# S5 outputs with the inputs and carried states as stationary operands and the tables streaming 128 columns

## The chip, the cores and the metric

The kernel runs on one core of a Trainium2 chip. The metric is device microseconds of one execution, the median over several runs. TensorE is called PE in the profile (its weight loads PEld), VectorE DVE, ScalarE ACT, GpSimd POOL and SyncE SP.

## What is computed

A trunk of four layers over 256 tokens of 1024 channels; layers 0 and 3 mix tokens with a diagonal state-space model (S5), layer 1 with differential attention, layer 2 with causal pooling, and each is followed by a squared-ReLU MLP. The change touches the S5 mixer alone:

```
u = h @ w_in                                  # 256 tokens, 64 groups of 16 channels
x_t = abar * x_(t-1) + bbar @ u_t             # 64 complex states per group, abar and bbar from the parameters
y_t = Re(c @ x_t) + d_skip * u_t
z = gelu(y)
out = (z * sigmoid(z @ w_gate)) @ w_out
```

## The kernel before, in words

Everything is float32. The S5 layer is cut into four quarters of the channels, each of 16 groups, taken as eight pairs of groups, and the 256 tokens into 64 chunks of four tokens. A pair of groups (2 x 16 channels) times four tokens makes 128 rows, so that a chunk's inputs are one column `V[:, :, j]` of a [128, 64] operand. For each quarter the kernel makes tables from the parameters: S takes a chunk's inputs to the state that they reach, T a chunk's inputs to its own outputs, and O the state before a chunk to its outputs.

`SEQ` is the order of emission, written out by hand, and the matmuls of the layer are pinned to it. Its letters, each with a quarter: `g` the product with w_in, `V` its result in rows of channels, `i`, `o`, `s` the tables on the vector and scalar engines, `S` and `T` what TensorE makes of the tables (S by transposes, T by 16 small products with a 32-column stationary operand, here called the T fill, evicted at L623 and copied into place at L626), `m` the states (`s5_state`, 16 matmuls of 64 columns), `c` the states carried over the chunks (`s5_chain`, on the vector engine, ending in `h`), `y` the outputs (`s5_out`), `z` transposes of the GELU's result, `e` the gate product, `w` the product with w_out. In layer 3 the tables come from memory, where `s5_put` kept them (K, H, L bring them back).

The stage `y` stands at L708 to L731. For each of the eight pairs j it issues one matmul with T as the stationary operand (128 columns) and V streaming 64 columns, then two with the halves of O as stationary operand (64 columns each) and the carried state `h` streaming 64 columns; the two O products write the lower and the upper 64 rows of the same result. A float32 matmul is two instructions on the engine, so a stage is 48 instructions. The GELU (L725) then writes Z, which the vector engine turns in blocks of 32 (L729) so that `s5_z` (L734) can transpose it on TensorE. `s5_chain` (L683) makes the phase table with three rows (minus sine, cosine, sine) so that one add makes both parts, and its last four adds write `h` with the two groups of a pair side by side, 64 partitions at a time; `s5_out_table` (L632) copies O into place in four pieces of 64 partitions.

Two pools matter: `m2` (11 buffers) and `m4` (12 buffers); results of TensorE rotate through eight banks.

Of the kernel before, what the change touches and what calls it, by code (L numbers as in the profile page):

```python
# [39 lines left out]
def plan():  # L40
    """Half blocks of 256 rows x 512 columns (array, index, row, column) in the order in which they are used."""
# [50 lines left out]
class Net:  # L92
# [69 lines left out]
    def exp(self, out, x, shape, tag):  # L162
        """exp on the vector engine: 2^n times a polynomial of the rest, its even and its odd terms apart."""
# [26 lines left out]
    def fetch(self):  # L190
        """Loads and splits the half blocks [128, 2, 512] that come next."""
# [23 lines left out]
    def mm3(self, out, sh, sl, mh, ml, start, stop):  # L215
        """out += (sh + sl)^T (mh + ml), of which sl^T ml is below float32's rounding."""
# [6 lines left out]
    def gemm_unit(self, xT, u, banks, first, last):  # L223
        """Both token tiles times a half block of 256 x 512."""
# [14 lines left out]
    def gemm_quarter(self, xT, bank, first, last):  # L239
        """Both token tiles times 512 x 256, side by side in one bank."""  # L240
# [14 lines left out]
    def gemm_T_unit(self, xT, u, banks, first, last):  # L255
        """banks[f // 2][:, f % 2] += (half block of 256 x 512)^T xT for its four column tiles f."""
# [18 lines left out]
    def operand(self):  # L275
        """Half of an operand [512 channels, 256 tokens]: rounded part and the rest."""
        return tuple(self.m4([128, 4, NT, 128], F32R) for _ in range(2))

    def split_T(self, xT, src, t, scale=None):
        """xT[:, q, t] = src[:, 128 q:]^T (times scale[:, q]) for four q, split."""  # L280
# [11 lines left out]
    def stat(self, t, n):  # L292
        """The squares of x[t][:, n half] towards the mean square; after both, 1 / rms."""
# [15 lines left out]
    def normed(self, n, t, sub, delay=1.5):  # L309
        """x[t][:, n half] is final for sublayer sub: its operands and statistics."""  # L310
# [11 lines left out]
    def first(self, n):  # L322
        """The same for a half of the input, in whole operands."""
# [80 lines left out]
    def rounded(self, out, a, s):  # L404
        """The integer nearest to a * s."""
# [7 lines left out]
    def s5_parts(self, l, P, q):  # L413
        tb = P[q]
        return [tb["O"], tb["T"], tb["ph"][:, 1:3], tb["rho"]]

    def s5_put(self, l, q):
        """Keeps the tables in memory until their layer."""
# [8 lines left out]
    def s5_get(self, l, q, part):  # L427
        """Brings back the tables of one stage: states and inputs (0), carries (1), outputs (2)."""
# [4 lines left out]
        elif part == 1:  # L433
            ph = self.t([128, 3, 8, 64], "ph", 2)
            P[q].update(ph=ph, rho=self.t([128, 8, 64], "rho", 2))
            a = [ph[:, 1:3], P[q]["rho"]]
        else:
            a = [self.O[q % 2], self.T[q % 2]]
        d = P["kept", q]
        for a, d in zip(a, d[2:4] if part == 1 else d[0:2]):  # L440
            self.nc.sync.dma_start(out=a, in_=d)
        if part == 1:
            self.nc.scalar.mul(ph[:, 0], ph[:, 2], -1.0)

    def s5_params(self, l, P):
        """The discretised parameters, [128 = two groups x 64 states, 32 pairs of groups]."""
# [46 lines left out]
        # powers 4 .. 0 of the discretised eigenvalues, and the factor of the inputs  # L493
# [11 lines left out]
        self.cmul(pr[:, 1], pi[:, 1], pr[:, 2], pi[:, 2], pr[:, 3], pi[:, 3], [sm(f"v{q}") for q in range(4)])  # L505
# [39 lines left out]
    def products(self, b, wa, wb):  # L545
        """b[0] times wa and b[1] times wb: b [128, 8, 16] over columns and powers, wa and wb [128, 8, 2, 4] over channels."""
# [8 lines left out]
    def s5_in_table(self, l, P, q):  # L555
        """From the inputs of a chunk to its state, for the eight pairs of groups 8 q .. (S)."""
# [21 lines left out]
    def swapped(self, l, q):  # L578
        """Whether the table of the states goes through memory to be turned."""
        return l == 1  # L580

    def s5_late(self, l, q, d=None):
        """The parts of the tables that the tensor engine makes: S from the inputs to the state, T to the outputs."""
# [47 lines left out]
    def s5_out_table(self, l, P, q):  # L631
        """From the state before a chunk to its outputs."""  # L632
# [10 lines left out]
        for x in range(2):  # L643
            yield
            self.halves(lambda g, p: nc.scalar.copy(O[64 * x:64 * x + 64, :, g],
                                                    d[p, :, x, 1:5].rearrange("p j k h -> p j (k h)")))
        P[q]["d"] = d

    def s5_small_tables(self, l, P, q):
        """Phases of the chunks, e^{4 i theta (c - 32)}, and the decay over a chunk, zero where a pair begins."""  # L650
# [11 lines left out]
        ph = self.t([128, 3, 8, 64], "ph", 2)  # L662
        nc.scalar.activation(out=ph[:, 0], in_=f, func=AF.Sin, scale=-turn)
        nc.scalar.activation(out=ph[:, 1], in_=a, func=AF.Sin, scale=-turn, bias=self.hpi[:, 0:1])
        nc.scalar.activation(out=ph[:, 2], in_=f, func=AF.Sin, scale=turn)
# [6 lines left out]
    def s5_state(self, l, P, q, V):  # L672
        """Eight pairs: the states that the chunks reach, from zero."""
        tb = P[q]
        tb["sb"] = []
        for ri in range(2):
            ps = self.bank()
            for j in range(8):
                self.mm(ps[:, 64 * j:64 * j + 64], self.st[q % 2][:, :, 2 * j + ri], V[:, :, j], start=True, stop=True)
# [3 lines left out]
    def s5_chain(self, l, P, q):  # L683
        """Eight pairs: the states carried over the chunks, before each chunk."""
# [6 lines left out]
        for a in range(2):  # L691
            self.tt(m[a], sb[a].unsqueeze(1).broadcast_to(S), turn[:, a:a + 2], ALU.mult)
        self.tt(m[0], m[0], m[1], ALU.add)
        G = self.m4(S)
        fl = lambda a: a.rearrange("p j c -> p (j c)")
        for a in range(2):
            nc.vector.tensor_tensor_scan(out=fl(G[:, a]), data0=fl(tb["rho"]), data1=fl(m[0][:, a]), initial=0.0,
# [3 lines left out]
        for a in range(2):  # L701
            self.tt(m[a][:, :, :, w], G[:, a, :, w].unsqueeze(1).broadcast_to([128, 2, 8, 63]),
                    turn[:, a:a + 2, :, w], ALU.mult)
        tb["h"] = h = self.m4(S)
        nc.gpsimd.memset(h[:, :, :, 0:1], 0.0)
        for g in range(2):
            for x in range(2):
                p = slice(64 * g, 64 * g + 64)  # L708
# [548 lines left out]
```

## Time and profile before

| | |
|---|---|
| median of three runs | 1205.5 us (1204.42 to 1205.73) |
| span of the profiled execution, first to last instruction | 1204.5 us |
| PE busy in it | 1171.1 us (97%) |
| DVE, ACT, POOL busy | 809.9, 663.4, 52.3 us |
| mean granted clock of TensorE | 0.953 of full |

The page prints the span of the profiled execution; its own time is not among the answers of the trace, and the three runs lie between 0.1 us below and 1.2 us above the span. Busy time of PE overlaps itself (the ends of matmuls are modelled), so a stage is measured here from its first start to the first start of the next stage.

### The profile page before, as it was taken

To read this page: it belongs to the slowest core of one execution; us is meant where nothing else is said; L and a number is where in the kernel's file an instruction comes from. 1 tells how busy PE (TensorE), PEld (TensorE's weight loads), DVE (VectorE), ACT (ScalarE), POOL (GpSimd) and SP (SyncE) were. 2 spreads that over 40 slices of the span, in tenths; PEclk is the share of its full clock that TensorE was granted. 3 is DMA by queue.
4 is the path that set the end of the run, shared out by engine and by line. 5 is a ranking of instruction groups with operands and counts; after the bars stand their busy time and mean duration, and the time that the engine had idled before them with its cause. 6 is when DMAs were issued, how large, how long until landed. Compare 5 with 4: busy or idle time off the path is not lost.

```text
span 1204.5 us, 18922 instructions
## 1 busy us (share of the span) xinstructions
PE 1171.1 (97%) x7192; PEld 1042.7 (87%) x7192; DVE 809.9 (67%) x1488; ACT 663.4 (55%) x1322; POOL 52.3 (4%) x111
## 2 busy tenths in 40 slices
PE   5999999999999999999999999999999999999994
PEld 4989889899888788989888899899898889989983
DVE  7766579857658997986655765655764766655563
ACT  4846367656656676775644754544630156554452
POOL 4002000000000001000000100000100001000000
PEclk9877799999999999999999999999985799999998
DMA  5211256766665444667667365665542256556651
GB/s 150 88 35 36 84 179 188 228 219 208 207 208 168 140 143 154 198 207 217 192 189 232 98 201 180 186 185 185 174 132 79 89 172 195 183 182 189 183 185 58
DMA packets 56635, 196.51 MB, mean 163 GB/s; under 512 B 7136, under 2 KB 7648, under 8 KB 56544
## 3 DMA queue, kind: packets, MB, share of 16 engines
q1 hardware_dynamic: 54528, 189.69, 50.5%
q10 hardware_dynamic: 2016, 5.61, 1.4%
q8 instruction: 56, 0.92, 0.3%
q14 instruction: 35, 0.29, 0.1%
HBM read 188.46 MB, written 6.82 MB: 162 GB/s over the span
## 4 chain that ended last, share of the span: by engine, by line
PE 94%; ACT 2%; DMA 1%; DVE 1%; issue 0%; SPq 0%; POOL 0%; ACTq 0%; POOLq 0%
PE mlp_ps L142 60%; PE mix_ps L142 31%; PE mix_ps L146 2%; DMA start_raw<-in_wts 1%; ACT start_st L598 0%; PE mlp_ps L146 0%; ACT mix_m L885 0%; ACT start_T L626 0%; ACT start_T L623 0%; DVE mix_m L151 0%; SPq L1071 0%; ACT mlp_m L1170 0%; DVE start_x L151 0%; ACT start_ba L575 0%; ACT mix_m L794 0%
## 5 line engine op out<-in xcount | busy, mean ns | idle before, releaser
L151 DVE TENSOR_TENSOR mlp_wlo<-mlp_raw,mlp_whi 128x512 fp32r<-128x512 f32 x492 | 318.5, 686 | 215.9 <-ACT mlp_whi L204 215.7
L204 ACT CAST mlp_whi<-mlp_raw 128x512 fp32r<-128x512 f32 x492 | 281.5, 618 | 255.3 <-PE mlp_ps L142 190.9
L142 PE MATMUL mlp_ps<-mlp_whi,mlp_m 128*128 128x512 f32 x1024 | 327.8, 396 | 0.0
L142 PEld LDWEIGHTS mlp_ps<-mlp_whi,mlp_m 128*128 128x128 f32 x1024 | 192.8, 188 | 45.5
L142 PE MATMUL mlp_ps<-mlp_m,mlp_whi 128*128 128x256 f32 x1248 | 226.2, 283 | 0.0
L142 PE MATMUL mlp_ps<-mlp_wlo,mlp_m 128*128 128x512 f32 x512 | 202.9, 396 | 0.0
L142 PEld LDWEIGHTS mlp_ps<-mlp_m,mlp_whi 128*128 128x128 f32 x1248 | 192.1, 188 | 0.6
L142 PE MATMUL mlp_ps<-mlp_m,mlp_wlo 128*128 128x256 f32 x624 | 175.2, 281 | 0.0
L142 PE MATMUL mlp_ps<-mix_m,mlp_whi 128*128 128x256 f32 x672 | 122.1, 283 | 0.0
L142 PEld LDWEIGHTS mlp_ps<-mlp_m,mlp_wlo 128*128 128x128 f32 x624 | 118.3, 190 | 0.0
L142 PEld LDWEIGHTS mlp_ps<-mlp_wlo,mlp_m 128*128 128x128 f32 x512 | 96.5, 188 | 22.0
L142 PE MATMUL mix_ps<-mix_whi,mix_m 128*128 128x512 f32 (+1 forms) x352 | 108.7, 385 | 0.0
L151 DVE TENSOR_TENSOR mix_wlo<-mix_raw,mix_whi 128x512 fp32r<-128x512 f32 x124 | 81.5, 685 | 38.4 <-ACT mix_whi L204 38.3
L204 ACT CAST mix_whi<-mix_raw 128x512 fp32r<-128x512 f32 x124 | 72.6, 621 | 62.0 <-PE mix_ps L142 35.0
L142 PEld LDWEIGHTS mlp_ps<-mix_m,mlp_whi 128*128 128x128 f32 x672 | 104.5, 188 | 1.8
L142 PE MATMUL mlp_ps<-mix_m,mlp_wlo 128*128 128x256 f32 x336 | 94.5, 281 | 0.0
L142 PEld LDWEIGHTS mix_ps<-mix_whi,mix_m 128*128 128x128 f32 x352 | 66.3, 195 | 13.3 <-issue 0.5
L142 PE MATMUL mix_ps<-mix_wlo,mix_m 128*128 128x512 f32 (+1 forms) x176 | 67.1, 381 | 0.0
L151 DVE TENSOR_TENSOR mlp_m<-mlp_m,mlp_m 128x512 fp32r<-128x512 f32 (+1 forms) x72 | 51.5, 716 | 19.4 <-ACT mlp_m L360 18.6
L142 PEld LDWEIGHTS mlp_ps<-mix_m,mlp_wlo 128*128 128x128 f32 x336 | 63.8, 190 | 0.0
L142 PE MATMUL mix_ps<-mix_m,start_st 128*128 128x64 f32 x256 | 56.9, 398 | 0.4 <-ACT start_st L598 0.3
L142 PEld LDWEIGHTS mix_ps<-mix_m,start_st 128*128 128x128 f32 x256 | 56.4, 311 | 0.9 <-ACT start_st L598 0.9
(324 smaller groups left out, 1523.5 us busy)
## 6 DMA issues: line engine op xcount, KB each, us to landing
mlp_raw<-in_wts SPq DMA_DIRECT2D x252, 512.0 KB, 4.1
mix_raw<-in_wts SPq DMA_DIRECT2D x84, 512.0 KB, 3.6
kept<-mlp_m SPq DMA_DIRECT2D x4, 512.0 KB
start_st<-kept SPq DMA_DIRECT2D x32, 64.0 KB, 3.3
start_x<-in_x SPq DMA_DIRECT2D x4, 256.0 KB
start_raw<-in_wts SPq DMA_DIRECT2D x2, 512.0 KB, 16.8
mlp_m<-in_s5bc SPq DMA_DIRECT2D x2, 512.0 KB, 4.6
kept<-start_O ACTq DMA_DIRECT2D x2, 512.0 KB
```

The lines of the kernel that those rows point to most:

```text
L142: i = self.nc.tensor.matmul(*a, **k)
L146: i = self.nc.tensor.transpose(*a)
L151: (eng or self.nc.vector).tensor_tensor(out=out, in0=a, in1=b, op=op)
L204: nc.scalar.copy(hi[:, s], raw[:, s])
```

## The change

In `s5_out` the roles are exchanged: for two pairs at a time (r = 0, 1) the inputs V of a pair and the two parts of its carried state `h` (64 columns each) are stationary, and T and O stream 128 columns. Pair r = 0 writes the lower 64 rows of the result, pair r = 1 the upper 64; the matmuls alternate between them. The number of matmuls stays 24 a quarter. The result now has chunks in rows, so the GELU writes in the order that the transposes of `s5_z` read, and the two DVE turns are gone. `V` and `h` get a layout in which a pair's 64 columns lie side by side; `h` is written by two adds over 128 partitions, the phase table loses its row of minus sines, and `s5_chain`'s one add of 1024 columns becomes two of 512. O is block-diagonal over the two groups, twice as large and zeroed once at the start by POOL; it is filled by two copies a quarter of twice the size, and kept in memory as two halves. The rows of w_gate and w_out are permuted on the host to match. `pe(...)`, which counts TensorE time for deferred work, gets 0.65 for a group of six matmuls in place of 0.43 for three.

```diff
@@ s5_parts
-        return [tb["O"], tb["T"], tb["ph"][:, 1:3], tb["rho"]]
+        return [tb["O"][0:64, 0], tb["O"][64:128, 1], tb["T"], tb["ph"], tb["rho"]]
@@ s5_get
-            ph = self.t([128, 3, 8, 64], "ph", 2)
...
-        if part == 1:
-            self.nc.scalar.mul(ph[:, 0], ph[:, 2], -1.0)
@@ s5_out_table
-        for x in range(2):
-            yield
-            self.halves(lambda g, p: nc.scalar.copy(O[64 * x:64 * x + 64, :, g],
-                                                    d[p, :, x, 1:5].rearrange("p j k h -> p j (k h)")))
+        yield
+        self.halves(lambda g, p: nc.scalar.copy(O[p, g].rearrange("p j x k -> p (j x) k"),
+                                                d[p].rearrange("p j x k h -> p (j x) (k h)")[:, :, 16:80]))
@@ s5_small_tables
-        ph = self.t([128, 3, 8, 64], "ph", 2)
-        nc.scalar.activation(out=ph[:, 0], in_=f, func=AF.Sin, scale=-turn)
...
@@ s5_state
-                self.mm(ps[:, 64 * j:64 * j + 64], self.st[q % 2][:, :, 2 * j + ri], V[:, :, j], start=True, stop=True)
+                self.mm(ps[:, 64 * j:64 * j + 64], self.st[q % 2][:, :, 2 * j + ri], V[:, j], start=True, stop=True)
@@ s5_chain
-        self.tt(m[0], m[0], m[1], ALU.add)
+        self.tt(m[0][:, 0], m[0][:, 0], m[1][:, 1], ALU.add)
+        self.tt(m[1][:, 0], m[1][:, 0], m[0][:, 1], ALU.subtract)
...
-        for g in range(2):
-            for x in range(2):
-                p = slice(64 * g, 64 * g + 64)
-                self.tt(h[64 * x:64 * x + 64, g, :, 1:64], m[0][p, x, :, w], m[1][p, x, :, w], ALU.add)
+        self.tt(h[:, 0, :, 1:64], m[0][:, 0, :, w], m[1][:, 1, :, w], ALU.subtract)
+        self.tt(h[:, 1, :, 1:64], m[1][:, 0, :, w], m[0][:, 1, :, w], ALU.add)
@@ s5_out
-        for j in range(8):
-            o = ps[:, 64 * j:64 * j + 64]
-            self.mm(o, tb["T"][:, j].rearrange("p g x -> p (g x)"), V[:, :, j], start=True, stop=False,
-                    skip_group_check=True)
-            for g in range(2):
-                self.mm(o[64 * g:64 * g + 64], tb["O"][:, j, g], tb["h"][:, g, j], start=False, stop=g == 1,
+        for i in range(4):
+            o = [ps[64 * r:64 * r + 64, 128 * i:128 * i + 128] for r in range(2)]
+            for r in range(2):
+                j = 2 * i + r
+                self.mm(o[r], V[:, j], tb["T"][:, j].rearrange("p g x -> p (g x)"), start=True, stop=False,
                         skip_group_check=True)
-            self.pe(0.43)
-        Z = self.m2([128, NT, 8, 32])
-        nc.scalar.activation(out=Z.rearrange("p t j c -> p j t c"),
-                             in_=ps.rearrange("p (j t c) -> p j t c", j=8, t=NT), func=AF.Gelu_apprx_tanh)
-        z = self.m2([128, NT, 2, 128])
-        for t in range(NT):
-            nc.vector.transpose(out=z[:, t].rearrange("p k (j h) -> p j k h", j=8),
-                                in_=Z[:, t].rearrange("p j c -> p (j c)"))
-        tb["z"] = z
+            for x in range(2):
+                for r in range(2):
+                    j = 2 * i + r
+                    self.mm(o[r], tb["h"][:, x, j], tb["O"][:, :, j, x], start=False, stop=x == 1,
+                            skip_group_check=True)
+            self.pe(0.65)
+        tb["z"] = z = self.m2([128, 4, 8, 16])
+        nc.scalar.activation(out=z.rearrange("p s j h -> p j s h"), in_=ps.rearrange("p (j s h) -> p j s h", j=8, s=4),
+                             func=AF.Gelu_apprx_tanh)
@@ build
-        self.O = [self.t([128, 8, 2, 64], f"O{b}") for b in range(2)]
+        self.O = [self.t([128, 2, 8, 2, 64], f"O{b}") for b in range(2)]
...
-        for a in (self.ba[0], self.T[0], self.ba[1], self.T[1]):
+        for a in (self.ba[0], self.T[0], self.O[0], self.ba[1], self.T[1], self.O[1]):
             nc.gpsimd.memset(a, 0.0)
```

How the instructions move. First PE at the first output stage of layer 0 (`m1`, `y0`, then the T fill of quarter 1). A row names the result, the streaming operand and the stationary one, and the shape of the result; `st` are the tables S, `m_125` is V and `m_154` the carried state. Before:

```order
L142 MATMUL mix_ps_585<-mix_m_127_437,start_st_18_96 128x64 x8
L142 MATMUL mix_ps_621<-mix_m_125_431,start_T_21_99 128x64
L142 MATMUL mix_ps_621<-mix_m_154_570,start_O_19_97 64x64 x2
L142 MATMUL mix_ps_653<-mix_cad_475,start_ba_16_94 32x64 x16
L142 MATMUL mix_ps_676<-mix_raw_356,mix_m_24_107 128x256 x8
```

and now:

```order
L142 MATMUL mix_ps_580<-mix_m_127_438,start_st_18_96 128x64 x8
L142 MATMUL mix_ps_615<-start_T_21_99,mix_m_125_432 64x128 x2
L142 MATMUL mix_ps_615<-start_O_19_97,mix_m_154_567 64x128 x4
L142 MATMUL mix_ps_644<-mix_cad_475,start_ba_16_94 32x64 x16
L142 MATMUL mix_ps_667<-mix_raw_358,mix_m_24_109 128x256 x8
```

The stages keep their order; the second and third row stand eight times before and four times now.

Second ACT behind that stage: the GELU of `y0` (L725, now L723), then the evictions of the T fill of quarter 1 (L623, now L620), the inputs V of quarter 2 (L794, now L786), the copies that the transposes of S need (`ba`), those that put T in place (L626, now L623) and the copies of S itself (`st`). Before:

```order
L725 ACTIVATE mix_m_167_646<-mix_ps_621 128x8x2x32
L623 ACTIVATE start_T_22_100<-mix_ps_653,start_gmask_83 32x8x64 x2
L575 COPY start_ba_15_93<-mix_m_158_596 64x64x16 x2
L794 ACTIVATE mix_m_177_700<-mix_ps_300,mix_rs_103_341 128x256
L638 COPY mix_cad_846<-mix_m_157_594 128x8x16
L598 COPY start_st_17_95<-mix_ps_705 128x4x128
L668 COPY mix_rho_966<-mix_q_rho_293 128x512
L626 COPY start_T_22_100<-start_T_22_100 32x16x48
```

and now:

```order
L723 ACTIVATE mix_m_167_640<-mix_ps_615 128x8x4x16
L620 ACTIVATE start_T_22_100<-mix_ps_644,start_gmask_83 32x8x64 x2
L786 ACTIVATE mix_m_176_689<-mix_ps_302,mix_rs_103_343 128x256
L635 COPY mix_cad_831<-mix_m_157_589 128x8x16
L572 COPY start_ba_15_93<-mix_m_158_591 64x64x16 x2
L623 COPY start_T_22_100<-start_T_22_100 32x16x48
L595 COPY start_st_17_95<-mix_ps_694 128x4x128
L663 COPY mix_rho_947<-mix_q_rho_295 128x512
```

T is put in place ahead of the copies of S, and the copies of `ba` now stand behind V and the copies into `cad`.

Third DVE, in the carries of quarter 1 (`c1`: the product with the second state part, then its adds and scans). Before:

```order
L151 TENSOR_TENSOR mix_m_161_604<-mix_ps_585,mix_ph_450 128x1024
L729 STREAM_TRANSPOSE mix_m_168_648<-mix_m_167_646 128x8x2x16
L151 TENSOR_TENSOR mix_m_160_603<-mix_m_160_603,mix_m_161_604 128x1024
L697 SCALAR_TENSOR_TENSOR mix_m_162_608<-mix_rho_454,mix_m_160_603 128x512 x2
L151 TENSOR_TENSOR start_T_22_100<-start_T_22_100,mix_dd_651 32x16x16
L151 TENSOR_TENSOR mix_m_165_615<-mix_m_163_611,mix_m_164_612 64x8x63 x4
```

and now:

```order
L151 TENSOR_TENSOR mix_m_161_599<-mix_ps_580,mix_ph_451 128x1024
L151 TENSOR_TENSOR start_T_22_100<-start_T_22_100,mix_dd_642 32x16x16
L151 TENSOR_TENSOR mix_m_160_598<-mix_m_160_598,mix_m_161_599 128x512
L693 SCALAR_TENSOR_TENSOR mix_m_162_604<-mix_rho_454,mix_m_160_598 128x512
L151 TENSOR_TENSOR mix_m_173_681<-mix_m_157_589,mix_q_pa_271 128x1024
L151 TENSOR_TENSOR mix_m_165_611<-mix_m_163_607,mix_m_164_608 128x8x63
```

The turns of `y0`'s result no longer stand ahead of `c1`'s adds; the add that finishes T of quarter 1 does.

## Rows read from the trace of the kernel before

**Rows 1.** The page: busy time, share of span and instructions of each engine
```profile
PE 1171.1 (97%) x7192; PEld 1042.7 (87%) x7192; DVE 809.9 (67%) x1488; ACT 663.4 (55%) x1322; POOL 52.3 (4%) x111
```
**Rows 2.** The page: the chain that ended last, by engine
```profile
PE 94%; ACT 2%; DMA 1%; DVE 1%; issue 0%; SPq 0%; POOL 0%; ACTq 0%; POOLq 0%
```
**Rows 3.** Windows: PE in the eight output stages y (us, busy, granted clock, DMA)
```profile
62.07:70.28 8.21, 8.21 (x49) 0.50 0.00 0
84.47:90.31 5.84, 5.84 (x48) 0.82 0.21 75
122.17:130.39 8.22, 8.22 (x50) 0.50 0.00 1
140.60:145.54 4.94, 4.94 (x51) 1.00 0.75 279
905.23:913.44 8.21, 8.21 (x49) 0.50 0.21 64
925.17:933.38 8.21, 8.21 (x49) 0.50 0.00 0
950.37:955.33 4.96, 4.96 (x49) 0.99 0.37 111
964.39:969.61 5.22, 5.22 (x51) 0.93 0.80 234
```
**Rows 4.** Timeline of PE: one pair of y0 (start, us, engine, line, out<-streaming,stationary)
```profile
63.05 0.69 PE L142 MATMUL mix_ps<-mix_m,start_T 128*128 128x64 f32 x2
63.67 0.48 PE L142 MATMUL mix_ps<-mix_m,start_O 128*64 128x64 f32 x4
64.08 0.69 PE L142 MATMUL mix_ps<-mix_m,start_T 128*128 128x64 f32 x2
```
**Rows 5.** Timelines cut short: matmuls started by 63.672 and 63.69, loads by 63.73
```profile
63.67 0.37 PE L142 MATMUL mix_ps<-mix_m,start_O 128*64 128x64 f32 x1
...
63.67 0.38 PE L142 MATMUL mix_ps<-mix_m,start_O 128*64 128x64 f32 x2
...
63.67 0.29 PEld L142 LDWEIGHTS mix_ps<-mix_m,start_O 128*64 128x64 f32 x3
```
**Rows 6.** Timeline of PE in attention: float32 matmuls of 128 streaming columns at full clock
```profile
446.48 1.06 PE L142 MATMUL mix_ps<-mix_m,mix_m 128*128 128x128 f32 x8
447.38 0.60 PE L146 MATMUL mix_ps<-start_ident,mix_m 128*128 128x128 f32 x4
```
**Rows 7.** Timeline of PE: the T fill of quarter 1 and of quarter 3, layer 0
```profile
70.28 3.62 PE L142 MATMUL mix_ps<-mix_cad,start_ba 128*32 128x64 f32 x32
...
110.93 1.97 PE L142 MATMUL mix_ps<-mix_cad,start_ba 128*32 128x64 f32 x32
```
**Rows 8.** Windows: first and last of six stretches behind output stages, all engines, and sum
```profile
70.28:74.58 4.30, 4.30 (x36) 4.04 (x35) 3.55 (x5) 1.24 (x3) 0.00 (x0) 0.50 0.00 0
...
969.61:972.28 2.67, 2.67 (x14) 2.67 (x13) 0.77 (x2) 0.60 (x1) 0.00 (x0) 0.50 0.57 204
sum 24.59, PE 24.59 PEld 22.46 DVE 14.54 ACT 5.97 POOL 0.00; mean PE 4.10 PEld 3.74 DVE 2.42 ACT 1.00 POOL 0.00
```
**Rows 9.** Groups by line and shape: the state matmuls of both layers
```profile
L142 PE MATMUL mix_ps<-mix_m,start_st 128*128 128x64 f32 x256 | 56.9, 398 | 0.4 <-ACT start_st L598 0.3
```
**Rows 10.** Timeline of ACT behind y0, and PE at y1 with its wait
```profile
75.10 2.08 ACT L575 COPY start_ba<-mix_m 64x1024 f32<-64x1024 f32 x2
77.20 0.84 ACT L794 ACTIVATE mix_m<-mix_ps,mix_rs 128x256 f32<-128x256 f32 x2
...
82.55 1.87 ACT L626 COPY start_T<-start_T 32x768 f32<-32x768 f32 x3
...
84.47 0.43 PE L142 MATMUL mix_ps<-mix_m,start_T 128*128 128x64 f32 x2 [1.37 <-ACT start_T L626]
```
**Rows 11.** Timelines of DVE (c1, and its wait for the GELU) and of POOL
```profile
71.03 0.45 DVE L729 STREAM_TRANSPOSE mix_m<-mix_m 128x256 f32<-128x256 f32 x1 [7.49 <-ACT mix_m L725]
...
2.52 0.95 POOL L1091 MEMSET start_T<- 128x1024 f32 x1
```

More of the change, by code (lines that the diff above doesn't have):

```diff
@@ L433, in s5_get @@
         elif part == 1:
-            ph = self.t([128, 3, 8, 64], "ph", 2)
-            P[q].update(ph=ph, rho=self.t([128, 8, 64], "rho", 2))
-            a = [ph[:, 1:3], P[q]["rho"]]
+            P[q].update(ph=self.t([128, 2, 8, 64], "ph", 2), rho=self.t([128, 8, 64], "rho", 2))
+            a = [P[q]["ph"], P[q]["rho"]]
         else:
-            a = [self.O[q % 2], self.T[q % 2]]
+            a = self.s5_parts(l, P, q)[0:3]
         d = P["kept", q]
-        for a, d in zip(a, d[2:4] if part == 1 else d[0:2]):
+        for a, d in zip(a, d[3:5] if part == 1 else d[0:3]):
             self.nc.sync.dma_start(out=a, in_=d)
-        if part == 1:
-            self.nc.scalar.mul(ph[:, 0], ph[:, 2], -1.0)
     def s5_params(self, l, P):
@@ L504, in s5_params @@
         self.tt(fi, t[2], t[3], ALU.subtract)
-        self.cmul(pr[:, 1], pi[:, 1], pr[:, 2], pi[:, 2], pr[:, 3], pi[:, 3], [sm(f"v{q}") for q in range(4)])
+        self.cmul(pr[:, 1], pi[:, 1], pr[:, 2], pi[:, 2], pr[:, 3], pi[:, 3], [sm(f"f{q}") for q in range(4)])
         yield
@@ L661, in s5_small_tables @@
         turn = 6.283185
-        ph = self.t([128, 3, 8, 64], "ph", 2)
-        nc.scalar.activation(out=ph[:, 0], in_=f, func=AF.Sin, scale=-turn)
-        nc.scalar.activation(out=ph[:, 1], in_=a, func=AF.Sin, scale=-turn, bias=self.hpi[:, 0:1])
-        nc.scalar.activation(out=ph[:, 2], in_=f, func=AF.Sin, scale=turn)
+        ph = self.t([128, 2, 8, 64], "ph", 2)
+        nc.scalar.activation(out=ph[:, 0], in_=a, func=AF.Sin, scale=-turn, bias=self.hpi[:, 0:1])
+        nc.scalar.activation(out=ph[:, 1], in_=f, func=AF.Sin, scale=turn)
         yield
@@ L691, in s5_chain @@
         for a in range(2):
-            self.tt(m[a], sb[a].unsqueeze(1).broadcast_to(S), turn[:, a:a + 2], ALU.mult)
-        self.tt(m[0], m[0], m[1], ALU.add)
+            self.tt(m[a], sb[a].unsqueeze(1).broadcast_to(S), turn, ALU.mult)
+        self.tt(m[0][:, 0], m[0][:, 0], m[1][:, 1], ALU.add)
+        self.tt(m[1][:, 0], m[1][:, 0], m[0][:, 1], ALU.subtract)
         G = self.m4(S)
@@ L696, in s5_chain @@
         for a in range(2):
-            nc.vector.tensor_tensor_scan(out=fl(G[:, a]), data0=fl(tb["rho"]), data1=fl(m[0][:, a]), initial=0.0,
+            nc.vector.tensor_tensor_scan(out=fl(G[:, a]), data0=fl(tb["rho"]), data1=fl(m[a][:, 0]), initial=0.0,
                                          op0=ALU.mult, op1=ALU.add)
@@ L701, in s5_chain @@
         for a in range(2):
-            self.tt(m[a][:, :, :, w], G[:, a, :, w].unsqueeze(1).broadcast_to([128, 2, 8, 63]),
-                    turn[:, a:a + 2, :, w], ALU.mult)
+            self.tt(m[a][:, :, :, w], G[:, a, :, w].unsqueeze(1).broadcast_to([128, 2, 8, 63]), turn[:, :, :, w],
+                    ALU.mult)
         tb["h"] = h = self.m4(S)
         nc.gpsimd.memset(h[:, :, :, 0:1], 0.0)
-        for g in range(2):
-            for x in range(2):
-                p = slice(64 * g, 64 * g + 64)
-                self.tt(h[64 * x:64 * x + 64, g, :, 1:64], m[0][p, x, :, w], m[1][p, x, :, w], ALU.add)
+        self.tt(h[:, 0, :, 1:64], m[0][:, 0, :, w], m[1][:, 1, :, w], ALU.subtract)
+        self.tt(h[:, 1, :, 1:64], m[1][:, 0, :, w], m[0][:, 1, :, w], ALU.add)
     def s5_out(self, l, P, q, V):
@@ L737, in s5_z @@
         pt = self.bank()
-        o = pt.rearrange("p (g t a k c) -> p g t a k c", g=2, t=NT, a=2, k=2)
-        for t in range(NT):
-            for k in range(2):
-                self.tr(o[:, :, t, :, k], z[:, t, k], self.ident)
-                self.pe(0.113)
+        o = pt.rearrange("p (a s c) -> p a s c", a=4, s=4)
+        for k in range(4):
+            self.tr(o[:, :, k], z[:, k].rearrange("p j h -> p (j h)"), self.ident)
+            self.pe(0.113)
         ks = slice(2 * (q % 2), 2 * (q % 2) + 2)
@@ L789, in step @@
             elif c == "V":
-                V[q] = self.m2([128, NT, 8, 32])
+                V[q] = self.m2([128, 8, 64])
                 u = self.m2([128, 512])
@@ L794, in step @@
                     nc.scalar.activation(out=u[:, s], in_=win[q][:, s], func=AF.Copy, scale=self.rstd[t])
-                    nc.vector.transpose(out=V[q][:, t].rearrange("p j c -> p (j c)"), in_=u[:, s])
+                    nc.vector.transpose(out=V[q][:, :, 32 * t:32 * t + 32], in_=u[:, s].rearrange("p (j c) -> p j c", j=8))
             elif c == "m":
@@ L1204, in lay_out @@
     wts = np.empty((len(blocks), 128, 1024), np.float32)
-    perm = np.arange(1024).reshape(4, 8, 2, 16).transpose(0, 2, 1, 3).ravel()
+    perm = np.arange(1024).reshape(4, 4, 2, 32).transpose(0, 2, 1, 3).ravel()
     for b, (name, i, r, c) in enumerate(blocks):
```

## The prediction

> **What bounds the kernel now.** First the page: PE is busy for 1171.1 us, 97% of the span [rows 1], and PE makes up 94% of the chain of work that ended last [rows 2]. So a microsecond that PE saves anywhere counts, unless PE then waits for something else; a microsecond that DVE, ACT or POOL saves counts only where PE waits for it. Second the windows of the eight output stages: together 53.8 us, but unequal for equal work. The second column of a window is the time, the fourth the granted clock: 8.21 us where it stands at 0.50 (TensorE at 1.2 GHz), 4.94 where it stands at 1.00 (2.4 GHz) [rows 3]. Five of the eight run wholly or partly at the lower level; y0 and y2 of layer 0 and y0 and y1 of layer 3 come right behind the state matmuls and run wholly at it.
>
> Third the inside of a stage. At the lower level a pair of groups takes 1.03 us: 0.62 us from the start of T's two instructions to O's first, 0.41 for O's four [rows 4]. So an O instruction takes a third of the time of one of T, and the cut timelines say why: the second O matmul starts less than 0.03 us behind the first, and three weight loads have begun within 0.06 us [rows 5]. They belong to the two halves of the array (lower and upper 64 rows of the result): **the halves work at the same time**. T's two instructions, 0.31 us each, compare with 3.62 us / 32 = 0.113 us each for the T fill, which also streams 64 columns at that level [rows 7]. The difference, 0.62 - 0.23 = 0.4 us, is what it costs to go from 64-column to 128-column stationary operands and back, eight times in a stage.
>
> **The change, part by part.**
>
> *The stage's matmuls.* Removed: 8 T and 16 O matmuls streaming 64 columns; added: 8 and 16 streaming 128, all with 64 stationary columns, alternating between the halves. The trace has no such stage. An instruction that streams 128 float32 columns is shown at the upper level in attention: eight from 446.48 to 447.38, 0.112 us each [rows 6]. That is the price for one half; at the lower level I double it, 0.224, which agrees with the T fill, 0.113 for half the columns [rows 7]. Per half there are 24 instructions: 24 x 0.112 = 2.69 us at the upper level, 5.38 at the lower. The bounds are 1 and 2 times this, as the halves overlap wholly or not at all; I take 1, since rows 5 show just this pair of halves overlapping. The change of shape stays once: 0.4 us at the lower level, 0.2 at the upper. So a stage costs **2.9 us** at the upper level, where it cost 4.95, and 5.8 at the lower, where it cost 8.21.
>
> *The clock.* Behind an output stage the lower level lasted on: six such stretches, from 2.67 to 5.62 us, 24.59 us in all, ran at 0.50 [rows 8]. They are T fill, transposes and large products that follow each other closely, and the level rose at the end of each. The old stage kept its halves idle for most of a pair (T's 0.62 us for two streams); the new one streams without a gap, as these stretches do, so I take it to raise the level as they did. Four stages start at the lower level. I take the rise 4.5 us into them, the middle of the longer stretches: (4.5 - 0.4) / 5.38 = 76% of the work at the lower level, the rest 0.24 x 2.69 = 0.65, in sum 5.15 us. The other four run at the upper level: 2.9. Sum 4 x 5.15 + 4 x 2.9 = 32.2, against 53.8: **21.6 us saved**. The bounds of this term are the level unchanged (the first rival) and 2.9 for all, 9 us more.
>
> *The stretches behind.* They now begin at the upper level. The T fill shows what that is worth: 1.97 instead of 3.62 us [rows 7]. Half of 24.59 is **12.3 us saved**; bounds 0 and 12.3.
>
> *ACT behind y0 of layer 0.* PE waited 1.37 us at y1 for T's copies (82.55, three, 1.87 us) [rows 10]. These now stand ahead of the copies of S, so that wait goes. But the copies of `ba` (2.08), for which PE's transposes of S wait, now stand behind V (0.84) and two small copies [rows 10], and PE arrives sooner: it has 16 instructions of product g in between, 3.5 us at the upper level, against 4.6 of ACT. I set a new wait of 1.1 against the old one of 1.37: nothing.
>
> *What costs nothing.* DVE loses two turns (0.45 us each [rows 11]) and shorter adds in each quarter, and no longer stands still behind the GELU (7.49 us before c1's adds [rows 11]); PE hid all that, and without this cover it would be some 2 us a quarter. ACT loses one Sine a quarter; its four copies of O become two of 64x1024, as long as one of `ba` (1.04 us [rows 10]). POOL zeroes O at the start: twice twice the 0.95 us of T [rows 11], 3.8 us, of which T of the second buffer waits 1.9; it is first filled near 50 us. O travels as two pieces of 256 KB, the bytes are the same. The transposes of z are as many and as large. Gone cover would cost 4 us at the start at most.
>
> **Sum.** 21.6 + 12.3 = 33.9; 1204.5 - 33.9 = 1170.6 us of span. The median of the runs shown is 1.0 us above this span, so the forecast is **1171.5 us**.
>
> **The rivals.**
>
> *The level does not rise (0.15).* For: a stage that follows the state matmuls began at 0.50 every time. Against: the T fill uses 32 of 128 columns and the level rose behind it all the same [rows 7, 8]. Then four stages take 5.8, the second of layer 0 (clock 0.82, 64% at the upper level) 3.9, the others 2.9, 2.9 and 3.2, in sum 36.1: 17.7 saved, nothing behind: 1188 us.
>
> *Loads in the open (0.06).* Each matmul would wait for its 64 columns of weights; rows 5 bound a load at 0.06 us, since with three begun by then one half has begun its second. 24 x 0.06 x 8 = 11.5 us more: 1183. Against: the third load had begun while the first matmul ran [rows 5]. The Trainium skill speaks for this rival on one page and against it on another: "TensorE: Matmul & The Clock Gate", Part 3, The mechanism, says that weight loads overlap running matmuls only when their row groups differ, and here both halves use all rows; "TensorEngine Tiling (Array Packing)", Key Properties, lets different tiles load and multiply in parallel. Rows 5 agree with the second. The second page also says that changing the tiling mode drains the array, which the 0.4 us above agrees with.
>
> *The halves take turns (0.05), slower.* Twice the columns and no overlap: 48 x 0.112 + 0.2 = 5.6 at the upper level, 48 x 0.224 + 0.4 = 11.2 at the lower. With the levels as before: 4 x 11.2 + 7.6 + 5.6 + 5.6 + 6.0 = 69.6, that is 15.8 lost: 1221 us. It would need the contention of 128-column streams, which no row shows. The point from which it decides: a pair of halves taking over (8.21 - 0.4) / 5.38 = 1.45 times one half's stream, with the level staying low.
>
> *The tables of layer 0 hold PE up (0.10).* From y0 to the T fill of quarter 2 PE comes some 8 us sooner, and ACT there worked almost without pause [rows 10]; c1 must go through T's add, two adds, two scans, two products and two adds on DVE before y1. If y1 and the fill each wait 3 us, 1177.5.
>
> *The state matmuls gain too (0.04).* They take 222 ns each (56.9 us / 256) [rows 9], twice the T fill's 113 with as many columns. Should the scattered halves of V be the cause, 256 x 0.109 = 28 us more would go: 1143.5. Against: T streamed the same V.
>
> **How the numbers follow.** The forecast has 0.60. The range of 8 in 10 reaches from 1163 (all stages at the upper level) to 1188 (the level does not rise); outside stay the state matmuls (0.04), the turns (0.05) and errors of price on both sides. About 0.2% is what a measurement of this kernel can tell from no change: faster by more 0.93, within it 0.02, slower 0.05.
>
> **What would show it.** In the profile after: output stages of 2.9 us at clock 1.00 and about 5.2 behind state matmuls; T and O as forms with 64 stationary and 128 streaming columns, starting in twos; the clock back at 1.00 in the first stretches behind y; no turn at L729; no wait of 1.37 us at y1, one near 1 us at the transposes of S behind y0. Wrong would be stages over 5.6 us at clock 1.00 (the halves take turns), clock 0.50 behind the stages, or PE waits of several microseconds in layer 0.

## The result and the profile after

The changed kernel takes 1173.71 us (median of four runs, 1171.43 to 1174.29), the kernel before 1204.96 (four runs, 1203.32 to 1205.73): a ratio of 0.9738, 95% interval 0.9723 to 0.9753. The forecast was 1171.5, in a range from 1163 to 1188. The profiled execution took 1174.07 us and spans 1171.9, against 1204.5: 32.6 us less, where the sum said 33.9.

First the page of the changed kernel: the busy times, and the chain of work that ended last by engine.

```profile
PE 1138.1 (97%) x7192; PEld 1019.7 (87%) x7192; DVE 795.9 (68%) x1464; ACT 655.2 (56%) x1296; POOL 65.7 (6%) x113
...
PE 94%; DMA 1%; ACT 1%; DVE 1%; POOL 1%; issue 0%; SPq 0%; ACTq 0%; DVEq 0%; POOLq 0%
```

PE is still the bound, with 33 us less of it [rows 1, 2]. New is POOL's share: it had none of the chain and now has 1%. Hold on to that; it is a wait that the forecast didn't see.

The eight output stages, as windows of PE (us, busy, granted clock, DMA):

```profile
63.83:68.83 5.00, 5.00 (x49) 0.54 0.00 0
80.60:84.89 4.29, 3.00 (x50) 1.00 0.45 122
115.53:120.28 4.75, 4.75 (x49) 0.57 0.01 2
127.82:130.59 2.77, 2.77 (x49) 1.00 0.84 248
889.66:894.75 5.09, 5.09 (x49) 0.53 0.37 103
904.72:909.13 4.41, 4.41 (x50) 0.62 0.00 0
924.86:927.64 2.78, 2.78 (x50) 1.00 0.88 258
935.18:937.95 2.77, 2.77 (x50) 1.00 0.86 278
sum 31.86, PE 30.57; mean PE 3.82
```

31.9 us in place of 53.8 [rows 3]. Stages that run wholly at the upper level take 2.77 us. Four start at the lower level, right behind the state matmuls, and now raise it on their way: if a stage starts at 0.50 and ends at 1.00, its mean clock tells when the level rose: (1 - 0.54) / 0.5 x 5.00 = 4.6 us into y0 of layer 0, and 4.1, 4.8 and 3.4 us into the others. The second window is the exception: PE is idle for 1.29 of its 4.29 us.

The inside of a stage, two pairs of groups at the lower and two at the upper level (timelines of PE), and a timeline that is cut short after 0.04 us:

```profile
65.17 0.64 PE L142 MATMUL mix_ps<-start_T,mix_m 128*64 128x128 f32 x4
65.59 1.07 PE L142 MATMUL mix_ps<-start_O,mix_m 128*64 128x128 f32 x8
...
128.53 0.39 PE L142 MATMUL mix_ps<-start_T,mix_m 128*64 128x128 f32 x4
128.75 0.61 PE L142 MATMUL mix_ps<-start_O,mix_m 128*64 128x128 f32 x8
129.18 0.39 PE L142 MATMUL mix_ps<-start_T,mix_m 128*64 128x128 f32 x4
...
128.53 0.28 PE L142 MATMUL mix_ps<-start_T,mix_m 128*64 128x128 f32 x2
```

From one T to the next 12 instructions pass in 0.65 us at the upper level: 0.109 us for each two. The cut timeline shows the twos: two matmuls have started within 0.03 us, and by the row above it only two more do in the next 0.2. These are the two halves of the array.

The stretches behind output stages (windows of PE: first and last of six that ran at the lower level before, and their sum; five are those of [rows 8], the other is the one behind y1 of layer 3):

```profile
68.83:73.13 4.30, 4.30 (x45) 1.00 0.00 0
...
937.95:940.60 2.65, 2.65 (x24) 1.00 0.77 207
sum 18.86, PE 18.86; mean PE 3.14
```

All six stand at clock 1.00, and so does the sixth of [rows 8], behind y2 of layer 3 (927.64 to 930.94 us). How much time that gave is read from start to start, since their ends moved:

| stretch (us, start to start) | before | after | saved |
|---|---|---|---|
| start of the program to the first state stage | 38.45 | 40.90 | -2.45 |
| from there to y0 of layer 0 | 23.62 | 22.93 | 0.69 |
| the eight output stages | 53.81 | 31.86 | 21.95 |
| the stretches behind seven of them (all but y3 of layer 0; waits included) | 294.63 | 281.85 | 12.78 |
| m2 to y2 of layer 0 | 27.39 | 28.25 | -0.86 |
| all else | 766.60 | 766.11 | 0.49 |
| span | 1204.5 | 1171.9 | 32.6 |

A stretch goes to the next state or output stage; the one behind y1 of layer 3 has a state stage in it, and the last runs to the end of the program.

Two lines of this table are losses, and the forecast has neither. The first is the clock again. Windows of PE between 15 and 25 us of the changed kernel, then the 16 matmuls there, before and now:

```profile
15.00:18.50 3.50, 3.50 (x11) 1.00 0.33 104
18.50:21.00 2.50, 0.01 (x1) 0.93 0.71 206
21.00:23.00 2.00, 1.65 (x4) 0.50 0.56 203
23.00:25.00 2.00, 2.00 (x7) 0.50 0.06 18
...
21.61 3.72 PE L142 MATMUL mix_ps<-start_raw,mix_m 128*128 128x256 f32 x16 [3.62 <-DMA start_raw<-in_wts]
...
21.36 6.73 PE L142 MATMUL mix_ps<-start_raw,mix_m 128*128 128x256 f32 x16 [2.85 <-DMA start_raw<-in_wts]
```

PE waits here for its first weights, and behind that wait the level falls to 0.50 for some seven microseconds; the kernel before stays at 1.00 there, behind a wait of 3.6 us. The 16 matmuls take 3.0 us longer; 0.55 us comes back, since the weights arrived 0.25 us sooner and PE did not wait 0.3 us for copies ahead of the first state stage. The second loss is that of the gate product behind m2, 5.96 us for 5.33, at a mean clock of 0.58 for 0.65 (0.63 of the 0.86 us). That leaves the 1.29 us inside y1 of layer 0. Timelines of PE, of POOL (this kernel, then the same product in the kernel before), and of DVE, around it:

```profile
80.60 0.44 PE L142 MATMUL mix_ps<-start_T,mix_m 128*64 128x128 f32 x4
82.33 0.66 PE L142 MATMUL mix_ps<-start_O,mix_m 128*64 128x128 f32 x8 [1.29 <-POOL mix_rho L664]
...
72.68 9.53 POOL L151 TENSOR_TENSOR mix_dd<-start_ident,start_dsk 32x256 f32<-32x256 f32 x1 [14.23 <-DVE start_T L151]
82.16 0.12 POOL L701 MEMSET mix_m<- 128x16 f32 x1
...
82.64 0.61 POOL L151 TENSOR_TENSOR mix_dd<-start_ident,start_dsk 32x256 f32<-32x256 f32 x1
...
81.67 0.43 DVE L787 STREAM_TRANSPOSE mix_m<-mix_m 128x256 f32<-128x256 f32 x1
```

The O matmuls need `h`, and the first column of `h` is zeroed by POOL (L701), which stands behind the product `dd` for T of the next quarter. That small product took 0.6 to 1 us before (once 5.7); here it lasts 9.53 us, and ends 0.5 us after DVE has begun a turn, about as long as it takes by itself. Up to that turn DVE had run operations with two inputs without a pause, from 72.5 us on. (The row names the memset of `rho`, the last on POOL; that of `h` is the one ahead of it.)

### The profile page after: what moved, and what is told of

Read it like the earlier page. It is cut to its first block, busy times and chain, and to the rows that moved or that the text cites. A ratio compares the mean times of both kernels' runs of the same rounds, so it can differ in the third digit from the quotient of the medians.

```text
span 1171.9 us, 18873 instructions
## 1 busy us (share of the span) xinstructions
PE 1138.1 (97%) x7192; PEld 1019.7 (87%) x7192; DVE 795.9 (68%) x1464; ACT 655.2 (56%) x1296; POOL 65.7 (6%) x113
## 4 chain that ended last, share of the span: by engine, by line
PE 94%; DMA 1%; ACT 1%; DVE 1%; POOL 1%; issue 0%; SPq 0%; ACTq 0%; DVEq 0%; POOLq 0%
PE mlp_ps L142 62%; PE mix_ps L142 29%; PE mix_ps L146 2%; DMA start_raw<-in_wts 1%; POOL mix_dd L151 1%; PE mlp_ps L146 0%; ACT mix_m L877 0%; ACT start_T L620 0%; DVE mix_m L151 0%; SPq L1063 0%; ACT mlp_m L1162 0%; DVE start_x L151 0%; ACT start_T L623 0%; ACT mlp_m L297 0%; DVE mix_wlo L151 0%
## 5 line engine op out<-in xcount | busy, mean ns | idle before, releaser
L142 PE MATMUL mix_ps<-mix_whi,mix_m 128*128 128x512 f32 (+1 forms) x352 | 106.3, 378 | 0.0
L204 ACT CAST mix_whi<-mix_raw 128x512 fp32r<-128x512 f32 x124 | 72.6, 620 | 55.0 <-PE mix_ps L142 31.9
L151 DVE TENSOR_TENSOR mlp_m<-mlp_m,mlp_m 128x512 fp32r<-128x512 f32 (+1 forms) x72 | 51.6, 717 | 20.1 <-ACT mlp_m L360 19.9
```

The lines of the kernel that those rows point to most:

```text
L142: i = self.nc.tensor.matmul(*a, **k)
L151: (eng or self.nc.vector).tensor_tensor(out=out, in0=a, in1=b, op=op)
L204: nc.scalar.copy(hi[:, s], raw[:, s])
```

## The experiments

Their common question: where the 22 us of the stages come from, what the new waits are, and what sets the 7.0 us of a state stage, behind which the level is low. All times stand beside 1173.71. The kernel before, measured again beside them, took 1206.46 us with one half of the experiments and 1205.37 with the other, against 1204.96 above, so differences up to some 1.5 us tell nothing. The diffs are shown shortened to what bears on the argument.

**One half at a time.**

```diff
-        for i in range(4):
-            for r in range(2): T of pair 2 * i + r
-            for x in range(2): for r in range(2): O of pair 2 * i + r
+        for r in range(2):
+            for i in range(4): T, O, O of pair 2 * i + r
```

> The changed kernel, but all twelve matmuls of the lower half first, then all twelve of the upper half; the same work. Theory (the gain is the overlap of the halves): in the changed kernel instructions start in twos, a pair of them every 0.109 us; one half at a time, 48 x 0.109 = 5.2 us a stage at the upper clock level, 10.5 at the lower. If the level still rises some 4.5 us into the four stages that start low, these take 7.5 in place of 4.8, the others 5.2 in place of 2.8: 20 us more, 1194. If one half alone does not raise the level, as in the kernel before, 4 x 10.5 + 4 x 5.2 = 63 and the 12 us behind the stages are lost too: 1217. Rival (128 streaming columns for 64 are the gain, the order of the halves is nothing): 1173.7, stages of 2.8 and 4.8 as now.

Measured: 1188.91 us (1187.51 to 1191.18), 15.2 more. Windows of four of its output stages, and a timeline where the lower half ends and the upper begins:

```profile
62.42:69.48 7.06, 7.06 (x50) 0.70 0.00 0
117.79:124.48 6.69, 6.69 (x49) 0.74 0.00 1
132.02:137.03 5.01, 5.01 (x50) 1.00 0.63 226
912.45:919.46 7.01, 7.01 (x50) 0.71 0.00 1
```
```profile
937.98 0.38 PE L142 MATMUL mix_ps<-start_T,mix_m 128*64 128x128 f32 x2
938.20 0.27 PE L142 MATMUL mix_ps<-start_O,mix_m 128*64 128x128 f32 x1
938.20 0.32 PE L142 MATMUL mix_ps<-start_T,mix_m 128*64 128x128 f32 x1
```

Within a half the instructions stand one behind the other, two in 0.22 us (937.98 to 938.20); only where the halves meet do an O and a T start together (the T is the upper half's first, and three more O stand ahead of it in the program). So a stage takes 46 x 0.109 = 5.01 us where the alternating one takes 2.77: **the overlap of the halves is worth 2.2 us a stage**, and the exchange of 64 streamed columns for 128 alone nothing (a stage took 4.95 before). The rival falls. The clock tells something else: the level rises here too, 3.5 to 4.2 us into the three low stages. It rose with one half at work at a time, streaming without a gap. From the low stages I had expected 7.5 us; the rise came sooner, and the eight stages of this profile sum to 49.0 us, 17 more than above where 20 had been expected. Of the rest, 1.7 us lies where the level was low for a shorter time than in the changed kernel's profile: the first state stage starts at 39.79 us, and the gate product behind m2 takes 5.35.

**The zeros of h on DVE.**

```diff
-        nc.gpsimd.memset(h[:, :, :, 0:1], 0.0)
+        nc.vector.memset(h[:, :, :, 0:1], 0.0)
```

> The changed kernel, but the zeros in the first column of h are written by DVE in place of POOL. Theory (POOL's product for T, 9.53 us where it took 0.61 before, is kept from running by DVE, and the zeros stand behind it on POOL, so PE waits 1.29 us in y1): the wait goes, 1172.4; POOL's product stays long. Rival (the carries themselves are late, and the zeros only came last): the wait stays under another name, 1173.7.

Measured: 1169.68 us (1168.14 to 1171.44), 4.0 less. The start of y1 on PE, and the product on POOL:

```profile
77.65 0.44 PE L142 MATMUL mix_ps<-start_T,mix_m 128*64 128x128 f32 x4
77.92 0.61 PE L142 MATMUL mix_ps<-start_O,mix_m 128*64 128x128 f32 x8
...
69.74 9.54 POOL L151 TENSOR_TENSOR mix_dd<-start_ident,start_dsk 32x256 f32<-32x256 f32 x1 [13.74 <-DVE start_T L151]
```

POOL is held for 9.54 us as before, but nobody waits: T and O follow each other without a pause. The wait of 1.29 us was POOL's; the carries were in time. The other 2.7 us of the median are not that wait. In the two profiles they lie where the level was low for a shorter time (the gate product behind m2 takes 4.83 us in place of 5.96, the first state stage starts at 39.13 and not 40.90); how much of that follows from the edit was not separated.

**The zeros of O on ACT.**

```diff
-        for a in (self.ba[0], self.T[0], self.O[0], self.ba[1], self.T[1], self.O[1]):
+        for a in (self.ba[0], self.T[0], self.ba[1], self.T[1]):
             nc.gpsimd.memset(a, 0.0)
+        for b in range(2): nc.scalar.copy(self.O[b], self.ba[0])
```

> The changed kernel, but O is zeroed by two copies on ACT in place of two memsets on POOL. Theory one (POOL's memsets hold up DVE between 7.2 and 9.8 us, and this puts the first state stage at 40.9 us where it stood at 38.5): DVE's short instructions there take 0.2 us each again, the first state stage stands near 38.5, 1171.3. Theory two (the 2.4 us are the clock's fall to 0.50 at 20.7 us, while PE waits for the weights, and whether it falls there hangs on the moment, not on POOL): DVE is free again but the first state stage comes at 38.5 or 41 according to the clock at 21 us, and the median stays within 1.5 us of 1173.7.

Measured: 1172.53 us (1172.42 to 1173.19), 1.2 less, within the spread of the changed kernel. DVE is free again: the instruction that stands at 10.85 us in the changed kernel stands at 8.26, as in the kernel before. But the first state stage starts at 40.47 us and the level falls at the start all the same:

```profile
18.50:21.00 2.50, 0.29 (x1) 0.77 0.86 281
21.00:23.00 2.00, 2.00 (x5) 0.50 0.22 78
```

So POOL's memsets do hold DVE up by 2.6 us, which the forecast had not seen, and it costs next to nothing, since DVE waits for ACT's sines behind it. They are not what the start lost. Theory two stands.

**The kernel before once more**, to see its start.

> The kernel before, unchanged, profiled once more, for the start alone. Theory one (the 2.4 us that the changed kernel lost up to its first state stage are the clock's fall at 21 us, which comes or not from execution to execution): m0 may start anywhere between 38.5 and 41 us, and the granted clock between 18 and 28 us says why. Theory two (something in the changed kernel causes it): m0 starts at 38.5 us again, with the clock at 1.00.

Measured: 1203.29 us for a span of 1201.5, first state stage at 38.29 us, and the clock between 18.5 and 23 us:

```profile
18.50:21.00 2.50, 0.00 (x0) 1.00 0.72 230
21.00:23.00 2.00, 1.54 (x7) 1.00 0.51 185
```

No fall in either profile of the kernel before. Of the changed kernel and its seven variants the level fell at this place in six executions (first state stage between 38.97 and 40.90 us) and not in two (37.48 and 38.69). The two without a fall have nothing in their start that the others lack, and PE's wait is 2.5 to 4.7 us long in the six, 2.8 and 3.7 in the two. So it most likely comes and goes from execution to execution. The changed kernel's own four runs fit that, from 1171.43 us at a mean clock of 0.973 to 1174.29 at 0.970, but only one of them was profiled. That the change makes the fall likelier, six of eight against none of two can't exclude.

**Two turns a quarter put back on DVE.**

```diff
+        turned = self.m2([128, 512])
+        for t in range(NT):
+            nc.vector.transpose(out=turned[:, 256 * t:256 * t + 256], in_=z[:, 256 * t:256 * t + 256])
```

> The changed kernel with the two turns of 0.45 us put back on DVE behind each GELU (they write a buffer that nobody reads, and take one more of the eleven). Theory (what DVE saves is hidden): within 1.5 us of 1173.7; the wait in y1 of layer 0, set by POOL, may move by 1 us. Rival (DVE's standstill behind the GELU makes the carries late, as it would have made them in the kernel before with a faster PE): PE waits 2 to 4 us more at y1 of layer 0 and up to 1 us in others, 1176 to 1180.

Measured: 1173.81 us (1172.83 to 1174.94): no difference, though not because nothing happens. From PE's waits and POOL's timeline:

```profile
PE mix_ps L142 <- ACT mix_m L749: 1.5, 1, 1.5
...
PE mix_ps L142 <- ACT start_T L623: 1.4, 1, 1.4
```
```profile
76.49 0.73 POOL L151 TENSOR_TENSOR mix_dd<-start_ident,start_dsk 32x256 f32<-32x256 f32 x1
```

The order on DVE is another one, and with it POOL's product runs beside a turn at 76.67 and takes 0.73 us. The wait for the zeros is gone, and so is that of 0.8 us for the copies of `ba`; in their place PE waits 1.4 us for T's copies ahead of y1, as in the kernel before [rows 10], and 1.5 us for an eviction of ACT at the gate product. One pair of waits for another: what DVE saves is not what the time is made of.

**h scattered.**

```diff
-        tb["h"] = h = self.m4([128, 2, 8, 64])
+        tb["h"] = self.m4([128, 2, 64, 8]); h = tb["h"].rearrange("p x c j -> p x j c")
```

> The changed kernel, but the 64 columns of a pair in h lie 32 bytes apart; V stays as it is. Theory (a scattered stationary operand costs 0.222 us for 128 columns at either clock level, so 0.111 for 64, and the loads of the two halves take turns): at the upper level a stage has 32 loads of 0.111 and 16 of 0.055, 4.4 us in place of 2.8; at the lower level 5.4 hides them. Four upper stages 1.6 each more, and the level rises later or not in the others, up to 5 us: 1180 to 1185. Rival (each half loads beside the other, within the 0.109 us of a matmul): 1173.7.

Measured: 1174.02 us (1172.43 to 1174.67): no difference to be told. The same place as in the second timeline above, a stage at the upper level:

```profile
125.20 0.39 PE L142 MATMUL mix_ps<-start_T,mix_m 128*64 128x128 f32 x4
...
125.90 0.38 PE L142 MATMUL mix_ps<-start_T,mix_m 128*64 128x128 f32 x4
```

T to T takes 0.70 us in place of 0.65, a stage 2.97 in place of 2.77. My theory had said 4.4 and falls: 64 columns 32 bytes apart are loaded almost within the 0.109 us of the matmuls beside them. The layout of `h` was worth 0.2 us in each upper stage, no more. The total hides two other things: this profile has no fall of the clock at the start, and PE waits 1.92 us for POOL's zeros in y1 and not 1.29.

**S in rows, layer 0.** Layer 3 fetches only the blocks on the diagonal of S and takes the zeros between them from what layer 0 left. In this kernel they lie elsewhere, so layer 3 multiplies other values there; its instructions, shapes and strides are those of the changed kernel.

```diff
-                nc.scalar.copy(st.rearrange("p m (j x) -> p j m x", x=2)[:, 4 * b:4 * b + 4, :, ri], ps)
+                nc.scalar.copy(st.rearrange("p (j x m) -> p x j m", x=2, m=128)[:, ri, 4 * b:4 * b + 4], ps)
```

> The changed kernel, but in layer 0 alone the tables S lie so that the 128 columns of a stationary operand are side by side in memory (they are 64 bytes apart). Theory (the 0.222 us of a state matmul, at either clock level, are the loading of a scattered stationary operand): in layer 0 they take 0.113 us and a state stage 3.6 us in place of 7.0, 4 x 3.4 = 13.6 us less, 1160; if the level then no longer falls in these stages, y0, y2 and the first gate product gain 6 more: 1154. Rival (the price is that of 128 columns for 64 streamed, wherever they lie): 7.0 us as now, 1173.7.

Measured: 1153.83 us (1153.00 to 1154.27), 19.9 less. The state stages of layer 0 take 3.5 us in place of 7.0:

```profile
77.69 3.68 PE L142 MATMUL mix_ps<-mix_m,start_st 128*128 128x64 f32 x32
81.21 3.67 PE L142 MATMUL mix_ps<-mix_m,mix_raw 128*128 128x256 f32 x16
```

32 instructions in 3.52 us (77.69 to 81.21), 0.110 each, where [rows 9] gave 0.222: **the price of the state matmuls was the loading of a stationary operand whose columns lie 64 bytes apart**. And the level stays up in them: the gate product behind m2 takes 3.5 us, where it took 5.96. PE reaches y1 sooner, so its wait for POOL's zeros grows to 2.29 us; behind that wait the level falls to 0.50 (72.33 to 75.05 us). The 19.9 us are what is left after this loss.

**S in rows in both layers**, with the zeros of `h` on DVE and those of O on ACT: the fastest version. S's turned blocks are kept and fetched with 32 columns side by side, in twice as many transfers.

```diff
-        self.st = [self.t([128, 128, 16], f"st{b}") for b in range(2)]
+        self.st = [self.t([128, 16, 128], f"st{b}") for b in range(2)]
...
-                nc.sync.dma_start(out=st[r:r + 16, 64 * g:64 * g + 64], in_=kept[2 * g:2 * g + 2, k % 2, :, k // 2])
+                for b in range(2):
+                    nc.sync.dma_start(out=st[r:r + 16, :, 64 * g + 32 * b:64 * g + 32 * b + 32], in_=kept[2 * g + b, k % 2, :, k // 2])
```

> The changed kernel with three edits: the tables S lie in rows of 128 side by side in both layers (layer 3 brings them from memory in pieces of 128 bytes, twice as many DMAs), the zeros of h are written by DVE, O is zeroed on ACT. Theory (the scattered stationary operand is the price of the state matmuls in both layers): layer 3 gains what layer 0 gained, 4 x 3.4 us in the stages and some 5 us of level in y0 and y1; with the 20 us of layer 0 and the 4 of the zeros 1173.7 - 20 - 18 - 4 = 1132. Rival (the fetch in small pieces comes late or SP's queue holds up the weights): PE waits in layer 3, 1140 to 1155.

Measured: 1129.28 us (1127.63 to 1129.55), a ratio of 0.9366 to the kernel before (0.9351 to 0.9380). A state and an output stage of layer 3, the transfers of S (KB each, us to landing), and the weight loads of the state matmuls (sum, mean ns), in the changed kernel and here:

```profile
851.46:855.07 3.61, 3.61 (x34) 1.00 0.85 284
855.07:857.84 2.77, 2.77 (x49) 1.00 0.73 191
```
```profile
start_st<-kept SPq DMA_DIRECT2D x64, 32.0 KB, 3.5
...
L142 PEld LDWEIGHTS mix_ps<-mix_m,start_st 128*128 128x128 f32 x256 | 56.3, 310 | 0.6 <-ACT start_st L595 0.5
...
L142 PEld LDWEIGHTS mix_ps<-mix_m,start_st 128*128 128x128 f32 x256 | 29.3, 192 | 0.1
```

They run at clock 1.00, and the mean granted clock of the execution is 0.994; a load lasts 192 ns in place of 310. A fetch lands in 3.5 us in place of 2.5, and PE waits for none.

## Why the prediction was right, and where it was off

*What bounds the kernel; the halves.* Right. The step from [rows 5] (three loads begun within 0.06 us) to "the halves work at the same time" carried the forecast, and the first experiment shows that it is the gain: 2.77 against 5.01 us. The price of 0.112 us for an instruction and half measured 0.109; the change of shape, put at 0.2 us a stage at the upper level, is 2.77 - 24 x 0.109 = 0.15.

*The clock.* Right in kind: the new stage raises the level. Taken was a rise 4.5 us into the low stages, 5.15 us each; they took 4.8 on average. The stage's term: 21.6 forecast, 21.95 measured, with 1.3 us lost in y1 already taken off. The reason given, that it streams without a gap, agrees with the first experiment, where the level rose with one half at work at a time. What kept it low in the old stage was not tried apart.

*The stretches behind.* 12.3 forecast, 12.8 measured, and part of that is the change of waits around y1's first stretch: 1.37 us gone, 0.79 come at the transposes of S, where 1.1 was set:

```profile
75.25 1.97 PE L146 MATMUL mix_ps<-start_ident,start_ba 128*128 128x128 f32 x16 [0.79 <-ACT start_ba L572]
```

*What costs nothing.* **This is the step that failed**: POOL's share was put at 3.8 us at the start, for the new memsets, and its old work was not looked at. T's add now stands ahead of c1's adds, so POOL's next product began just as the carries began on DVE, with no turn between them; it was held for 9.5 us, and the zeros of `h` behind it kept PE 1.29 us. The rival that the tables of layer 0 hold PE up (3 us at y1 and 3 at the T fill) had the place of the first and the wrong engine, and the second did not come. The Trainium skill has a mechanism that fits: "SBUF — State Buffer", SBUF: two separate sides, says that DVE and GpSimd share a pair of ports that one of them holds for a whole instruction while the other is blocked, among other cases when DVE's instruction has two inputs in SBUF and GpSimd's reads SBUF. The trace agrees and goes further: the product was kept out over all of DVE's instructions from 72.7 to 81.7 us, and ended only once the first turn had begun. That DVE's instructions kept it out rests on this order of events, and on the 0.73 us that it took in another order, with two turns put back; that the ports are the reason was not tried apart.

*The sum.* 33.9 against 32.6 of span: the stages and stretches gave 34.7, m0 to y0 and the rest 1.2, the start took 2.45 (3.0 by the fall of the clock, 0.55 given back) and the stretch from m2 to y2 0.86. The forecast has no term for either, so part of its nearness is luck: 3.3 us of losses without a term stand against 1.2 of gains without one and 0.8 by which the stages and stretches did better. A further 0.9 us is the offset (1170.6 + 1.0 is 1171.6, which the forecast gave as 1171.5): the sum took the runs to lie 1.0 us above the span, but the median lies 1.8 us above it; a run and its own span differ by 2.2 us (1174.07 and 1171.9), and by 1.8 in the second profile of the kernel before. The profile of before had been set against the median of other executions.

*The rivals.* The level did rise. The halves do not take turns. Loads do not stand in the open: even scattered they add 0.2 us a stage. The loads of O's weights begin at 128.64 us, while T's matmuls run from 128.53 to 128.92 (timeline of the loads, at the place shown above):

```profile
128.64 0.47 PEld L142 LDWEIGHTS mix_ps<-start_O,mix_m 128*64 128x64 f32 x8
```

Of the two pages of the Trainium skill that the prediction set against each other, "TensorEngine Tiling (Array Packing)", Key Properties, agrees with these runs; the rule of "TensorE: Matmul & The Clock Gate", Part 3, The mechanism, that loads overlap only where the row groups differ, doesn't hold for two halves of the columns. Both halves used all rows, and in each a load of 64 columns went with each 0.109 us of matmul. The state matmuls did not gain (57.0 us in their group, 56.9 before), so V was not their cause, as argued; the stride of S was. The Trainium skill, "Advanced Engine Details and Errata", SBUF Cachelines, has a rule that fits: lines of 16 bytes, and a penalty when each access takes another line. Columns 64 bytes apart cost double here; 32 bytes apart, with 64 columns for each half, only 0.2 us a stage. Why so much less was not tried.

## What to carry to other kernels

Where a matmul uses half of the array's columns, alternate two of them, instruction by instruction: the halves overlapped only as near neighbours in the program, and the same matmuls in blocks took 1.8 times as long. Keep the columns of a stationary operand side by side; a group whose time doesn't follow the clock (the state stages took 6.9 to 7.2 us at mean clocks from 0.76 to 0.88) is not bound by the matmul, and here the level fell in it and stayed low in what followed. When a change moves work on DVE, read POOL's timeline again as well: what stood there in short pauses may find none.

## What was not expected of the hardware

- POOL's product of 32x256 took 0.6 to 1 us in the kernel before (5.68 once), 9.53 us behind DVE's two-input operations without a pause, and 0.73 us beside a turn. The other way round, POOL's memsets of 1.8 us held short DVE instructions of 0.2 us for up to 1.75.
- The level fell at 21 us, behind PE's wait for weights, in six of ten profiled executions and not in the other four, with waits of like length (2.5 to 4.7 us, and 2.8 to 3.7). It fell as well behind the wait of 2.29 us in y1 of layer 0 with S in rows there, and not at the same place behind 1.29 us (changed kernel) and 1.92 us (`h` scattered).
- With the halves in blocks, the first T of the upper half began with an O of the lower half (938.20 us) ahead of three more O that stand before it in the program.
- The level rose in output stages with one half of the array at work at a time. In the state stages at 0.222 us an instruction, with the whole array, it fell each time (clock 0.76 to 0.88 over the stage); at 0.110 us an instruction it didn't.
